# Channel shuffle in place: eight 24 KB buffers replaced by three 64 KB buffers with half-buffer stores

## The chip, the core and the metric

The kernel runs on one core of a Trainium2 chip. The metric is the device time of one execution in microseconds. A core has several engines that run side by side, each with its own instruction stream; here VectorE (DVE) and ScalarE (ACT) compute, and SyncE (SP) issues loads. ACT also issues the stores. The transfers themselves are done by 16 DMA engines, which take their work from one queue filled by SP and one filled by ACT.

## What is computed

The input has 16 x 64 x 64 rows of 256 channels in float32, 67.1 MB. In each row the 256 channels, 8 groups of 32, are transposed to 32 groups of 8. No arithmetic is done; every byte is read once from HBM and written once to it.

```
x = x.reshape(batch, h, w, groups, channels_per_group)   # groups 8, channels_per_group 32
x = x.transpose(0, 1, 2, 4, 3)
x = x.reshape(batch, h, w, c)
```

## The kernel before

A row of 256 channels is 1 KB, and there are 65,536 of them. A *tile* of size q is 128 x q consecutive rows: partition p holds the q rows that start at row p x q of the tile, so that each partition reads and writes one contiguous run of q KB. `_SIZES` (L12) lists 22 tiles: twenty of 24, one of 8, one of 24. They sum to 512, and 512 x 128 rows are the whole input.

Each tile takes one buffer of 24 KB a partition from a pool of eight (L13, L37, L49), 192 KB a partition in all. SP loads it with a single DMA (L50). Then, in pieces of 8 rows (8 KB a partition, `_PIECE`, L15), VectorE copies the piece to a PSUM tile called `bounce` and permutes it on the way (L54), and ScalarE copies `bounce` back over the same place in the buffer (L58). The PSUM pool has two such tiles. After the last piece of a tile, ACT issues a single DMA that stores the whole buffer (L59).

The instructions stand on each engine in the order in which they are written (the schedule is manual). Waits between engines are semaphores that the framework sets. SP can load tile i+8 when the store of tile i has landed, because it goes into the same buffer. All DMAs, loads and stores, share eight completion semaphores; a DMA that is to use one also waits until the DMA that used it before has landed. An engine that waits holds up everything behind it on its own stream: when ACT waits to issue a store, its next copies wait too, and with two PSUM tiles VectorE soon after.

Of the kernel before, what the change touches and what calls it, by code (L numbers as in the profile page):

```python
# [1 line left out]

# [4 lines left out]


F32 = mybir.dt.float32
P = 128  # L10

_SIZES = [24] * 20 + [8, 24]  # L12
_BUFS = 8  # L13

_PIECE = 8  # L15


@with_exitstack
def kernel(
    ctx: ExitStack,  # L20
    tc: tile.TileContext,
    x: bass.AP,
    groups: bass.AP,
    out: bass.AP,
):
    nc = tc.nc
    b, h, w, c = x.shape
    G = int(groups)
    CPG = c // G
    assert G * CPG == c  # L30
    assert sum(_SIZES) * P == b * h * w
    biggest = max(_SIZES)

    x_flat = x.rearrange("b h w c -> (b h w c)")
    out_flat = out.rearrange("b h w c -> (b h w c)")

    pool = ctx.enter_context(tc.tile_pool(name="pool", bufs=_BUFS))  # L37
    psum = ctx.enter_context(
        tc.tile_pool(name="psum", bufs=2, space=bass.MemoryType.PSUM)
    )  # L40

    def rows(flat, first, q):

        return flat[first * c : (first + P * q) * c].rearrange("(p f) -> p f", p=P)

    ctx.enter_context(tc.manual_schedule(engines=None))
    first = 0
    for q in _SIZES:
        buf = pool.tile([P, biggest * c], F32, name="buf")  # L49
        nc.sync.dma_start(out=buf[:, : q * c], in_=rows(x_flat, first, q))  # L50
        for k in range(0, q, _PIECE):
            piece = buf[:, k * c : (k + _PIECE) * c]
            bounce = psum.tile([P, _PIECE * c], F32, name="bounce")
            nc.vector.tensor_copy(  # L54
                out=bounce.rearrange("p (i j g) -> p i j g", j=CPG, g=G),
                in_=piece.rearrange("p (i g j) -> p i j g", g=G, j=CPG),
            )
            nc.scalar.copy(out=piece, in_=bounce)  # L58
        nc.scalar.dma_start(out=rows(out_flat, first, q), in_=buf[:, : q * c])  # L59
        first += P * q  # L60


# [1 line left out]
_INS = ['x', 'groups']  # L64
_OUTS = [((16, 64, 64, 256), 'float32')]

_NUMBERS = {'groups': 8}


# [26 lines left out]
```

## Time and profile before

| What | us |
|---|---|
| median of 4 runs | 317.55 |
| lowest and highest run | 317.46 and 317.63 |
| the profiled execution | 317.46 |
| its span, first to last recorded event | 315.7 |
| L54, VectorE copy, 64 of 3.637 us each | 227.9 busy, 72.2 idle before it |
| L58, ScalarE copy, 64 of 1.866 us each | 119.0 busy, 170.7 idle before it |
| L50, load of 3 MB, issue to landing, median of 21 | 59.4 |
| L59, store of 3 MB, issue to landing, median of 21 | 24.6 |
| first and last issue of a load | 0.7 and 241.8 |
| first and last issue of a store | 23.7 and 302.0 |

The profiled execution's time is 1.8 us more than its span; this much lies around what the profile records. The time from issue to landing of a DMA includes the time it stood in its queue behind earlier ones. The page gives a row of DMA shares, one digit for each of 40 slices of the span (9 is 90% or more of the 16 engines' time), and counts packets: a packet is what a DMA engine moves in one go. Besides the data, each DMA sends one packet of 4 bytes on each engine, which raises its completion semaphore. The view by windows cuts the span into stretches and gives the busy time and the number of instructions of each engine, the clock, the DMA share and the rate in GB/s of each; the DMA view does so for queues, where q1 holds the loads and q10 the stores. A packet is counted in the window in which it starts.

### The profile page before, as it was taken

The page shows a single profiled execution, that of the slowest core. Times are in us where ns is not written, and L with a number is a line of the kernel's source. Part 1 is how long each engine was busy: PE and PEld are TensorE (multiplying, and loading weights), DVE is VectorE, ACT ScalarE, POOL GpSimd, SP SyncE. Part 2 cuts the span into 40 slices and gives each one's busy share as a digit, 9 for nine tenths or more (in the row PEclk, how much of TensorE's full clock was granted, in tenths as well). Part 3 has the DMA queues.
Part 4 walks back from the last instruction along what each step waited for, and adds up shares of the span by engine and source line. Part 5 has one row for each costly group of instructions (what it writes and reads, how often), then busy time and mean ns, then how long its engine had stood idle before and what let it go on. Part 6 is the DMA issues. An engine that isn't in the chain of part 4 may idle for free.

```text
span 315.7 us, 289 instructions
## 1 busy us (share of the span) xinstructions
DVE 227.9 (72%) x64; ACT 120.3 (38%) x65; POOL 0.2 (0%) x4
## 2 busy tenths in 40 slices
DVE  0699999959586685957008986999970299999900
ACT  0354455524252424330015426545500444554420
POOL 0000000000000000000000000000000000000000
DMA  8999999999999999999999999999999999999997
GB/s 302 436 439 392 424 439 433 424 439 439 417 439 442 417 436 442 417 439 445 417 439 437 420 439 436 430 430 434 433 430 433 436 430 431 431 439 427 430 432 315
DMA packets 6338, 134.24 MB, mean 425 GB/s; under 512 B 704, under 2 KB 704, under 8 KB 704
## 3 DMA queue, kind: packets, MB, share of 16 engines
q1 hardware_dynamic: 3168, 67.11, 49.9%
q10 hardware_dynamic: 3168, 67.11, 49.4%
q14 instruction: 2, 0.02, 0.0%
HBM read 67.11 MB, written 67.11 MB: 425 GB/s over the span
## 4 chain that ended last, share of the span: by engine, by line
DVE 54%; another core or an unknown queue 23%; issue 8%; ACT 5%; DMA 3%; DVEq 1%; ACTq 0%
DVE bounce L54 54%; ACT buf L58 5%; DMA buf<-in_x_dram 3%; DVEq L91 1%; ACTq L59 0%; DVEq L54 0%; ACTq L58 0%
## 5 line engine op out<-in xcount | busy, mean ns | idle before, releaser
L54 DVE COPY bounce<-buf 128x2048 f32<-128x2048 f32 x64 | 227.9, 3637 | 72.2 <-ACT buf L58 38.4
L58 ACT COPY buf<-bounce 128x2048 f32<-128x2048 f32 x64 | 119.0, 1866 | 170.7 <-DVE bounce L54 115.3
L58 ACT ACT_TABLE_LOAD x1 | 1.3, 1283 | 11.1 <-DMA buf<-in_x_dram 11.1
L77 POOL MEMSET const-bfloat16-1.0<- 128x1 bf16 x1 | 0.1, 101 | 0.0
L77 POOL MEMSET const-uint8-127<- 128x1 uint8 x1 | 0.1, 101 | 0.0
L77 POOL MEMSET const-float32-0.0<- 128x1 f32 x1 | 0.1, 98 | 0.2 <-issue 0.2
L77 POOL MEMSET const-float32-1.0<- 128x1 f32 x1 | 0.1, 98 | 0.0
## 6 DMA issues: line engine op xcount, KB each, us to landing
buf<-in_x_dram SPq DMA_DIRECT2D x21, 3072.0 KB, 59.4
out_dram<-buf ACTq DMA_DIRECT2D x21, 3072.0 KB, 24.6
buf<-in_x_dram SPq DMA_DIRECT2D x1, 1024.0 KB, 44.9
out_dram<-buf ACTq DMA_DIRECT2D x1, 1024.0 KB, 16.1
```

What stands on the lines that cost most here:

```text
L54: nc.vector.tensor_copy(out=bounce.rearrange("p (i j g) -> p i j g", j=CPG, g=G), in_=piece.rearrange("p (i g j) -> p i j g", g=G, j=CPG),)
L58: nc.scalar.copy(out=piece, in_=bounce)
L77: nc = _bacc.Bacc("TRN2", target_bir_lowering=False, num_devices=1)
L91: with _tile.TileContext(nc) as tc:
```

## The change

The tiles become one of 16, one of 32, seven of 64 and one of 16 rows a partition (again 512 in all). The pool has three buffers of 64 KB a partition, again 192 KB. Each tile is still loaded by one DMA. The pieces stay 8 rows, and what VectorE and ScalarE do with a piece stays the same. A store now covers 32 rows (`_STORE`): ACT issues it after the copies of its four pieces, so that a tile of 64 is stored by two DMAs, the first while the second half is still to be permuted. There are 10 loads and 17 stores instead of 22 and 22.

```
-_SIZES = [24] * 20 + [8, 24]
-_BUFS = 8
+_SIZES = [16, 32] + [64] * 7 + [16]
+_BUFS = 3
+
+_STORE = 32
...
     for q in _SIZES:
         buf = pool.tile([P, biggest * c], F32, name="buf")
         nc.sync.dma_start(out=buf[:, : q * c], in_=rows(x_flat, first, q))
-        for k in range(0, q, _PIECE):
...
+        for a in range(0, q, _STORE):
+            b = min(a + _STORE, q)
+            for k in range(a, b, _PIECE):
+                piece = buf[:, k * c : (k + _PIECE) * c]
+                bounce = psum.tile([P, _PIECE * c], F32, name="bounce")
+                nc.vector.tensor_copy(
+                    out=bounce.rearrange("p (i j g) -> p i j g", j=CPG, g=G),
+                    in_=piece.rearrange("p (i g j) -> p i j g", g=G, j=CPG),
+                )
+                nc.scalar.copy(out=piece, in_=bounce)
+            cols = slice(a * c, b * c)
+            nc.scalar.dma_start(
+                out=rows(out_flat, first, q)[:, cols], in_=buf[:, cols]
             )
-            nc.scalar.copy(out=piece, in_=bounce)
-        nc.scalar.dma_start(out=rows(out_flat, first, q), in_=buf[:, : q * c])
         first += P * q
```

SP can now load tile i+3 when both stores of tile i have landed. The eight completion semaphores are shared as before.

More of the change, by code (lines that the diff above doesn't have):

```diff
@@ L26 @@
     nc = tc.nc
-    b, h, w, c = x.shape
+    n, h, w, c = x.shape
     G = int(groups)
@@ L30 @@
     assert G * CPG == c
-    assert sum(_SIZES) * P == b * h * w
+    assert sum(_SIZES) * P == n * h * w
     biggest = max(_SIZES)
@@ L50 @@
         nc.sync.dma_start(out=buf[:, : q * c], in_=rows(x_flat, first, q))
-        for k in range(0, q, _PIECE):
[L52 to L56, printed above, removed]
-            )
-            nc.scalar.copy(out=piece, in_=bounce)
-        nc.scalar.dma_start(out=rows(out_flat, first, q), in_=buf[:, : q * c])
+        for a in range(0, q, _STORE):
[11 more added lines that the diff above has]
+                out=rows(out_flat, first, q)[:, cols], in_=buf[:, cols]
+            )
         first += P * q
```

## The prediction

> **What bounds the kernel now.** I read the page first: busy shares, then the row of DMA shares, then the queues.
>
> ```profile
> span 315.7 us, 289 instructions
> DVE 227.9 (72%) x64; ACT 120.3 (38%) x65; POOL 0.2 (0%) x4
> ...
> DMA  8999999999999999999999999999999999999997
> ...
> DMA packets 6338, 134.24 MB, mean 425 GB/s; under 512 B 704, under 2 KB 704, under 8 KB 704
> ## 3 DMA queue, kind: packets, MB, share of 16 engines
> q1 hardware_dynamic: 3168, 67.11, 49.9%
> q10 hardware_dynamic: 3168, 67.11, 49.4%
> ```
>
> VectorE, the busiest engine, idles for 28% of the span; the DMA engines never do (two queues, 49.9% + 49.4%). The chain of waits ends on VectorE (54%) all the same, because it cannot see a queue that is merely full. The view by windows shows where DMA time is lost:
>
> ```profile
> core 0: us, DVE busy (x) ACT busy (x) POOL busy (x), PEclk, DMA share, GB/s
> 0.00:4.00 4.00, 0.00 (x0) 0.00 (x0) 0.20 (x4) 1.00 0.63 184
> 4.00:24.00 20.00, 12.96 (x4) 6.88 (x4) 0.00 (x0) 1.00 1.00 433
> 24.00:32.00 8.00, 8.00 (x3) 3.73 (x2) 0.00 (x0) 1.00 1.00 390
> 32.00:156.00 124.00, 92.98 (x27) 46.63 (x25) 0.00 (x0) 1.00 1.00 432
> 156.00:164.00 8.00, 0.00 (x0) 0.00 (x0) 0.00 (x0) 1.00 1.02 439
> 164.00:172.00 8.00, 5.32 (x2) 5.27 (x3) 0.00 (x0) 1.00 1.00 431
> ...
> 286.00:304.00 18.00, 14.12 (x4) 9.27 (x5) 0.00 (x0) 1.00 0.99 427
> 304.00:314.00 10.00, 0.00 (x0) 0.00 (x0) 0.00 (x0) 1.00 0.97 415
> 314.00:315.70 1.70, 0.00 (x0) 0.00 (x0) 0.00 (x0) 1.00 0.00 0
> ```
>
> The last column is the rate. It is about 432 GB/s with both queues (32 to 156), 433 with loads alone (4 to 24), and 431 with stores alone (the DMA view for 288 to 313.5). So 134.22 MB need 310.3 us, whichever queue supplies them. Losses are shortfalls against 432: (432 - 184)/432 x 4 = 2.3 us at the start, 0.8 us when the first store sets in (24 to 32), 0.2 + 0.4 us near the end, and 1.7 us after the last byte. 310.3 + 5.4 = 315.7, the span: nothing else is left to win.
>
> So the change can help only by cheaper bytes or smaller losses, and it hurts wherever **both** queues run empty at once. To foresee that I need the rule by which they share. The DMA view for 262 to 271, when an 8 KB tile loads beside 24 KB stores:
>
> ```profile
> DMA packets 264, 3.89 MB, mean 432 GB/s; under 512 B 21, under 2 KB 21, under 8 KB 21
> ## 3 DMA queue, kind: packets, MB, share of 16 engines
> q10 hardware_dynamic: 132, 2.85, 73.6%
> q1 hardware_dynamic: 132, 1.04, 27.3%
> ```
>
> 132 packets against 132: the queues take turns by packet, not by byte, and a packet is one partition's row. The queue with the longer rows gets more.
>
> **The change, part by part.**
>
> *Fewer, longer packets.* Now: (6338 - 704 - 2)/16 = 352 data packets an engine. Then: 10 loads and 17 stores, (10 + 17) x 128/16 = 216. In the view above, without the 4-byte ones, 1.04 MB are 127 packets of 8 KB and 2.85 MB are 116 of 24 KB. 8 KB takes 27.3% of 16 x 9 us by 127 = 309 ns; 24 KB takes 73.6% by 116 = 914 ns. Three times 309 is 927, so a packet has a fixed cost of (927 - 914)/2 = 6.5 ns; the shares sum to 100.9%, so the packets overlap a little and I take 5. 136 x 5 ns = **0.7 us less** (bounds 0 and 136 x 8 = 1.1).
>
> *DMA issues.* SP issues 10 loads of 0.33 us instead of 22, ACT 17 stores of 0.34 us instead of 22. Both wait most of the time: nothing.
>
> *Start.* Tiles of 16 and 32 rows are queued at once with the first 64: 14.7 MB, 34 us of transfers, so the queue is full whatever VectorE does. VectorE starts some 2.4 us earlier (1.05 MB less to wait for), which nothing awaits. The losses of 2.3 and 0.8 us stay.
>
> *Three buffers in place of eight.* Load i+3 waits on SP for both stores of tile i; behind it stand only later loads. With 64 KB against 32 KB rows, loads get two thirds (288 GB/s) and stores one third (144). One cycle, from the landing of a tile's second store: its buffer's new load (8.39 MB) takes 29.1 us, in which one half store (4.19 MB) passes; then the load queue is empty (no buffer free), and the next half store has the engines alone for 9.7 us. It frees the next buffer. That is 38.8 us a tile, exactly 16.78 MB at 432: no idle time. VectorE needs 8 x 3.56 = 28.4 us a tile (a step is 10.7/3), so it waits 10 us each cycle for a load, hidden by the transfers.
>
> *The end*, where the buffering decides. When the last 64-row load lands, three half stores are still unsent by that cycle: 12.6 MB. Behind them come the last load (2.1 MB) and the final stores. The last tile's first half is due at (12.6 + 2.1)/0.432 = 34 us after that landing and ready after 0.4 + 3.6 + 3 x 3.56 + 1.9 = 16.6 us (landing to VectorE, four copies, ACT's last); the second half due at 43.7, ready at 30.8; the last tile due at 53.4, ready at 37.9. A store needs some 1 to 4 us from issue to first byte (the first load's 1; the first store was issued at 23.7 and the dip ends by 29). Slack is 9 us or more everywhere: no gap.
>
> *A lost stall.* The chain shows "another core or an unknown queue" with 22.8%; its longest piece, 25.5 us before 164.3, is ACT holding a store for a DMA semaphore of an earlier transfer (eight are shared by all transfers). DMA ran at full share meanwhile, so dropping it returns nothing. In the new order the transfer that held the same semaphore is always long landed.
>
> *Restarts*, the unknown. The load queue now runs empty and starts again beside stores six times (every big tile but one, and the last). Before has no such restart. Nearest rows: the store queue's restart after 164 (431 against 432, under 0.1 us) and its first start (0.8 us). Six times that: 0 to 4.7 us; a gain is excluded, since a queue that starts adds no rate. I take 0, as a restart is like the row at 164, not like a first start.
>
> Sum: the profiled execution's 317.46 - 0.7 = 316.75. That execution lies 0.09 under the median of 317.55; I forecast **316.8**.
>
> *Two rules of the Trainium skill against rows.* The trace runs the only tile with a power-of-two row pitch, 8 KB, at 309 ns a packet, full rate. "DMA: Bandwidth & Descriptors", section "Latency and other measured facts", speaks against this change: copies lose rate at large power-of-two HBM row pitches, 207 GB/s at 512 KiB against 214 in full; 64 KB rows are new such pitches. Were that 3% paid here, the time would be about 327; at an eighth of that pitch I don't expect it, and no row here shows it. Its section "Bandwidth" gives 341 GB/s at 1 MB and 425 at 16 MB (transfers issued by GpSimd), which would promise much for larger DMAs; the rows here show 432 with 3 MB ones, since they queue back to back.
>
> **The rivals.**
>
> 1. *Slower: a 64 KB row is moved as two packets of 32 KB.* Rows up to 24 KB are one packet here; none of 64 KB is shown. Then the queues share equally, and loads no longer run ahead. The same bookkeeping leaves 6.2 MB unsent when the last big load lands; the last tile's second half is due at (6.2 + 2.1 + 4.2)/0.432 = 28.9 us but ready at 30.8 and on the wire 1 to 3 us later: 2.8 to 4.5 us with both queues empty. Net with 56 more packets: 317.5 + 2.8 or 4.5 - 0.4 = 319.8 to 321.5, likeliest 319.8. It decides as soon as less than some 8 MB is unsent then.
> 2. *Restarts cost part of the first start's price*, 0.1 to 0.8 us each: 317.3 to 321.4. Against it: the row at 164.
> 3. *Nothing measurable.* Packets have no fixed cost, or 0.3 us is lost elsewhere: 316.9 to 317.6. For it: 5 ns comes from a difference of 13 in 927.
> 4. *More than forecast.* Smaller first tiles also shrink the dip at the first store (0.8 us): 315.9 to 316.3.
>
> That the change doesn't do what it says is out: in the order of instructions every half store stands right after its fourth copy.
>
> **How the numbers follow.** No gap and packets cheaper, 316.3 to 317.1: 0.62. Rival 1: 0.12. Rival 2: 0.11. Rival 3: 0.07. Rival 4: 0.06. Rows above 24 KB, of which the trace shows none, move at a lower rate: 0.02. A measurement of this kernel tells about 0.2% (0.64 us) from no change, so the line lies at 316.9, inside the forecast's band: I count 0.45 of its 0.62 as faster. With rival 4 that makes 0.51. Same: the other 0.17, rival 3, 0.02 of rival 2: 0.26. Slower: 0.23. The range runs from rival 4's 315.9 to 320.0, leaving out the upper part of rivals 1 and 2; the restarts' far end, 321.4, lies in that part.
>
> **What would show it.** Right: 27 x 128 data packets; a big load landing some 29 us after it begins, and beside it twice the stores' bytes; load queue empty for some 10 us per tile; windows at 432 to 434 from 32 to 310; VectorE waiting for loads about 10 us a tile. Wrong: more packets with equal bytes in both queues and an empty slice near 298 (rival 1); dips each time a load follows stores alone (rival 2); under 430 throughout (long rows at a lower rate).

## The result, and the profile after

The changed kernel takes 317.89 us (median of 42 runs) where the kernel before takes 317.61 (63 runs beside it): a ratio of 1.0014, interval 1.0007 to 1.002. That is 0.3 us slower, where 0.8 us faster was forecast. It lies inside the bound of 0.2% that I had called "same", but on the wrong side of the ratio 1. The changed kernel's runs also lie further apart: 37 of them from 317.2 to 318.7 and five from 319.3 to 323.2, where before stays within 317.3 and 318.1. The run of 323.2 counts as slow, and the ratio leaves it out. The profiled execution took 317.88.

From the page of the changed kernel, the span, packets and queues:

```profile
span 316.1 us, 235 instructions
...
DMA packets 3890, 134.24 MB, mean 425 GB/s; under 512 B 432, under 2 KB 432, under 8 KB 432
## 3 DMA queue, kind: packets, MB, share of 16 engines
q1 hardware_dynamic: 1440, 67.11, 49.8%
q10 hardware_dynamic: 2448, 67.11, 49.2%
```

1440 load packets are 10 x (128 + 16): a row of 64 KB is one packet. (3890 - 432 - 2)/16 = 216 data packets an engine, as forecast. From the DMA view of the same kernel for 56 to 100 us:

```profile
q1 hardware_dynamic: 215, 13.04, 68.4%
q10 hardware_dynamic: 216, 6.03, 31.7%
```

215 packets against 216, and twice the bytes: the queues do take turns by packet. The chain of waits shows the cycle that follows from it (start, duration, what):

```profile
108.21 42.05 DMA out_dram<-buf
...
150.73 38.64 another core or an unknown queue
...
189.83 38.58 another core or an unknown queue
...
228.46 0.04 issue
228.50 32.99 DMA buf<-in_x_dram
```

Loads of big tiles are issued near 150.4, 189.5 and 228.5, some 39 us apart, where 38.8 was forecast. The schedule is the one that was forecast. Yet 0.7 us were to be won and 0.4 were lost in this execution (317.88 against 317.46). Where, the view by windows tells roughly and the DMA view exactly. First the windows, of before and then of after:

```profile
60.00:300.00 240.00, 178.80 (x51) 92.87 (x50) 0.00 (x0) 1.00 1.00 432
...
312.00:313.00 1.00, 0.00 (x0) 0.00 (x0) 0.00 (x0) 1.00 1.03 442
313.00:314.00 1.00, 0.00 (x0) 0.00 (x0) 0.00 (x0) 1.00 0.35 147
314.00:315.00 1.00, 0.00 (x0) 0.00 (x0) 0.00 (x0) 1.00 0.00 0
```

```profile
60.00:300.00 240.00, 188.57 (x54) 100.72 (x54) 0.00 (x0) 1.00 1.00 433
...
312.00:313.00 1.00, 0.00 (x0) 0.00 (x0) 0.00 (x0) 1.00 0.99 426
313.00:314.00 1.00, 0.00 (x0) 0.00 (x0) 0.00 (x0) 1.00 0.84 360
314.00:315.00 1.00, 0.00 (x0) 0.00 (x0) 0.00 (x0) 1.00 0.04 16
```

In the middle the changed kernel is a little faster, and at the end it is half a microsecond late all the same. So most was lost before 60 us. There the time of one load packet tells it: the share of the queue, times 16 engines and the window, over the data packets. Of the kernel before, the DMA view for 25 to 30 us and for 100 to 105:

```profile
q1 hardware_dynamic: 61, 1.45, 82.1%
...
q1 hardware_dynamic: 45, 1.11, 51.3%
```

1.45 MB are 59 packets of 24 KB, 0.821 x 80/59 = 1.11 us each; normal is 0.513 x 80/45 = 0.91. So each engine lost 0.20 x 59/16 = 0.74 us just after the first store: this is the dip that the prediction had seen. Of the changed kernel, 36 to 41, 46 to 54 and 64 to 72:

```profile
q1 hardware_dynamic: 18, 1.05, 55.8%
...
q1 hardware_dynamic: 32, 2.10, 74.6%
...
q1 hardware_dynamic: 36, 2.36, 68.0%
```

A 64 KB packet takes 2.79, 2.98 and (normal) 2.42 us: 16 and 32 packets with 0.37 and 0.56 us too much, 0.4 + 1.1 = **1.5 us** lost an engine instead of 0.74. The larger part comes after the load of 42.8 us, the first that is issued to a load queue already empty: its first restart. From 18 to 36 us, already beside the first store (issued at 17.5), a load packet takes the normal 2.42 (80.7% of 18 us for 96 packets); the smaller dip comes shortly before that store ends.

Five more restarts follow in this profile, and they cost nothing. For 154 to 162 us, after the load of 150.4:

```profile
q1 hardware_dynamic: 47, 3.08, 88.8%
```

That is 0.888 x 128/47 = 2.42 us a packet again; the windows after the other four give 2.42 and 2.43, and 0.61 for the last load's 16 KB.

### The profile page after: what moved, and what is told of

Its sections match the earlier page's. It is cut to its first block, busy times and chain, and to the rows that moved or that the text cites. A ratio compares the mean times of both kernels' runs of the same rounds, so it can differ in the third digit from the quotient of the medians.

```text
span 316.1 us, 235 instructions
## 1 busy us (share of the span) xinstructions
DVE 227.8 (72%) x64; ACT 120.7 (38%) x65; POOL 0.2 (0%) x4
## 2 busy tenths in 40 slices
DMA packets 3890, 134.24 MB, mean 425 GB/s; under 512 B 432, under 2 KB 432, under 8 KB 432
## 3 DMA queue, kind: packets, MB, share of 16 engines
q1 hardware_dynamic: 1440, 67.11, 49.8%
## 4 chain that ended last, share of the span: by engine, by line
DMA 45%; another core or an unknown queue 24%; DVE 21%; ACT 2%; DVEq 1%; issue 0%; SPq 0%
DMA buf<-in_x_dram 24%; DMA out_dram<-buf 21%; DVE bounce L58 21%; ACT buf L62 2%; DVEq L98 1%; SPq L52 0%; DVEq L58 0%
```

## The experiments

Names of the theories: **A**, the dip belongs to the first stores; **B**, a load queue that has run dry restarts unevenly beside stores; **C**, the dip belongs to a place in the load queue; **D**, chance; **L**, long packets cost by themselves.

**Both kernels once more**, without an edit.

> The kernel before, once more, for its profile. In the first profile 0.7 us of each DMA engine's time is lost to slow load packets between 26 and 29 us, just after the first store is issued (23.7). Theory A, the price belongs to the first store: the dip is there again, at 26 to 29 us, 0.6 to 0.8 us. Theory C, it belongs to a place in the load queue (its 26th to 31st packet on each engine): the same place and size. Theory D, it is chance: another place, or another size by more than 0.3 us.

> The changed kernel, once more, for its profile. In the first profile 1.6 us is lost in two dips, 0.4 us at 37 to 39 us and 1.2 us at 46 to 53 us, the latter where the load queue starts again beside stores for the first time. Theory B, the first restart costs about 1 us: the second dip is there again, after 46 us, 1.0 to 1.4 us. Theory C: both dips at the same load packets (26th, 28th and 29th). Theory D: they move, or change by more than 0.4 us.

Before: 317.46 again, the rate over 4 to 60 us 428 GB/s as in the first profile, and the dip in its old place and size (25 to 30 us: 79.2% for 57 data packets, 1.11 us each). After: 318.25, but lost elsewhere. The windows do not tell where: 60 to 300 us has 431 GB/s where the first profile had 433, but 4 to 60 has 437 where that had 425, and 4 to 300 has 432 in both. A packet is counted in the window in which it starts, and one more of 64 KB on each engine is 1 MB. The DMA view for 47 to 55 us, where the first restart falls, for 115 to 123 and for 232 to 240:

```profile
q1 hardware_dynamic: 32, 2.10, 62.5%
...
q1 hardware_dynamic: 32, 2.10, 62.1%
...
q1 hardware_dynamic: 35, 2.29, 66.2%
```

A load packet takes 2.50, 2.48 and 2.42 us. The first restart costs 0.2 us here, not 1.1; the three after it some 0.1 each (154 to 162 and 193 to 201 have 61.9% and 61.6% for 32 packets); the last two nothing. The dip at 36 to 41 is there again, 0.4 us. So B's figure for the second dip (1.0 to 1.4) did not come, and neither did C's; for that dip D holds.

What ends last in this profile is one engine. In 41 to 42 us 15 engines send the 4-byte packet that closes the third load, and one sends it in 43 to 44, before the first restart (load issued at 44.8). At the end, 314.5 to 315.5 us, one engine still begins a 16 KB packet when the 15 others have closed the last store:

```profile
q1 hardware_dynamic: 15, 0.00, 0.8%
...
q1 hardware_dynamic: 1, 0.00, 0.1%
...
DMA packets 2, 0.02 MB, mean 16 GB/s; under 512 B 1, under 2 KB 1, under 8 KB 1
```

Its last packet starts at 315.2 us, 0.9 after that of the next to last engine; in the first profile all 16 close the third load within 0.8 us. The record does not name the engines, so it is not shown that the late one is the same each time.

**The stores of the kernel before, three tiles late.**

```
     first = 0
+    late = []
...
-        nc.scalar.dma_start(out=rows(out_flat, first, q), in_=buf[:, : q * c])
+        late.append((rows(out_flat, first, q), buf[:, : q * c]))
+        if len(late) > 3:
+            to, of = late.pop(0)
+            nc.scalar.dma_start(out=to, in_=of)
         first += P * q
+    for to, of in late:
+        nc.scalar.dma_start(out=to, in_=of)
```

> The kernel before, with each store issued three tiles later, so that the first one goes out after the copies of the fourth tile, near 56 us instead of 23.7; the transfers stay the same and the queues stay full, so the time should be that of before within 0.3 us. Theory A: no dip at 26 to 29 us, and one of about 0.7 us at 57 to 62. Theory C: the dip stays at 26 to 29 us although no store is in flight. Theory D: a dip somewhere else.

317.67 us, ratio 0.9999 (0.999 to 1.0008). The DMA view for 25 to 30 us and for 54 to 59:

```profile
q1 hardware_dynamic: 94, 2.24, 103.8%
...
q1 hardware_dynamic: 63, 1.47, 82.5%
```

0.91 us a packet (91 of them carry data) and 1.10 (60): the dip has gone from 25 us and come to 54 with the first store, at the same price, 0.19 x 60/16 = 0.7 us. A holds for the kernel before; C falls.

**The changed kernel with each load in two.**

```
-        nc.sync.dma_start(out=buf[:, : q * c], in_=rows(x_flat, first, q))
+        for a in range(0, q, _STORE):
+            cols = slice(a * c, min(a + _STORE, q) * c)
+            nc.sync.dma_start(out=buf[:, cols], in_=rows(x_flat, first, q)[:, cols])
```

> The changed kernel with each load of 64 rows issued as two DMAs of 32 rows. Packets are then 32 KB on both queues, 256 and 16 an engine instead of 200 and 16; at 5 ns each that is 0.3 us more than the changed kernel. The queues share equally and the load queue never runs dry, since VectorE starts on the first half while the second is loading. Theory B: the 1.2 us of the first restart goes, so the time is about 0.9 us under the changed kernel's, near 317.0, 0.998 of before. Theory A: the time is that of before less 0.4 us, 317.2, with one dip of 0.7 us near 20 to 24 us. Theory C: a dip at the load queue's 26th to 31st packets, here at about 30 to 45 us, and the time 317.2 to 317.9. If the load packets of 64 KB themselves cost something, rates in the middle go from 434 to 433 and nothing else changes.

317.23 us, ratio 0.9993 (0.9981 to 1.0005), where the changed kernel has 1.0014 (1.0007 to 1.002). With neither 64 KB packets nor a dry queue, and 56 more data packets an engine (272 against 216), most of the loss is gone. A had said 317.2 and B 317.0, so the time does not tell them apart; the only dip is the one that A has, 0.5 us at 20 to 31 us (61.3% of 11 us for 82 packets, 1.32 us each instead of 1.21). In 60 to 300 us:

```profile
60.00:300.00 240.00, 178.02 (x51) 93.11 (x51) 0.00 (x0) 1.00 1.01 434
```

**Tiles of 48 in four buffers**, stored whole, and then in halves.

```
-_SIZES = [16, 32] + [64] * 7 + [16]
-_BUFS = 3
+_SIZES = [16, 32] + [48] * 9 + [16, 16]
+_BUFS = 4
-_STORE = 32
+_STORE = 48      # in the second version 24
```

> The changed kernel with nine tiles of 48 rows in four buffers (192 KB as before) instead of seven of 64 in three, each stored by one DMA. Both queues then have 48 KB packets and share equally; the load queue never runs dry. 208 data packets an engine, 0.7 us less than before. Theory B (a load queue that has run dry starts again beside stores unevenly, and the last of the 16 engines sets the end): nothing is given back, 316.9, 0.998 of before. Theory L (long packets are themselves uneven, dry queue or not): as the changed kernel, 317.7 to 318.2.

> The same tiles of 48 rows in four buffers, but stored in two DMAs of 24 rows each. Loads get two thirds again and the load queue runs dry eight times, some 8 us each. 288 data packets an engine, 0.3 us less than before. Theory B: eight restarts at 0.1 to 0.2 us give 0.8 to 1.6 us back, 318.1 to 318.9. Theory L: shorter store packets than in the version stored whole, so no worse than it plus 0.4 us. If neither costs anything: 317.3.

Whole: 320.21 us, 1.0078 (1.0052 to 1.0103); in halves: 318.36, 1.0031 (1.0015 to 1.0048). For the first, neither B's 316.9 nor L's 317.7 to 318.2 came, and it tells less than I wanted: in its profile (318.69) the store queue ran dry too, with no store packet from 287.1 to 289.3 us. The profiled execution of the second, 317.43, was its fastest, so it does not show what made the others slower. But it has the dry load queue eight times, and that cost it nothing. From 76.2 to 80.9 us only stores move; from 80 to 88, after the restart, a 48 KB load packet takes 0.683 x 128/48 = 1.82 us, as in a version below whose load queue does not run dry:

```profile
q10 hardware_dynamic: 88, 2.04, 100.7%
...
q1 hardware_dynamic: 48, 2.36, 68.3%
```

The windows after the next five restarts have 68.1% or 68.2% for 48 packets, and after the last two a 16 KB packet takes its normal 0.61 us. A restart beside stores need not cost anything.

**Tiles of 32 in six buffers.**

```
-_SIZES = [16, 32] + [64] * 7 + [16]
-_BUFS = 3
+_SIZES = [16] + [32] * 15 + [16]
+_BUFS = 6
```

> Fifteen tiles of 32 rows in six buffers (192 KB), each loaded and stored by one DMA, tiles of 16 first and last. 32 KB packets on both queues, 272 an engine, 0.4 us less than before; the load queue never runs dry. Theories B and L both: 317.2 to 317.4, 0.9985 to 0.999 of before, as with the changed kernel's split loads.

317.05 us, ratio 0.998 (0.9972 to 0.9989): this version beats both kernels. 434 GB/s in the middle, and the engines end together (0.99, then 0.12):

```profile
60.00:300.00 240.00, 178.00 (x51) 93.03 (x51) 0.00 (x0) 1.00 1.01 434
...
312.00:313.00 1.00, 0.00 (x0) 0.00 (x0) 0.00 (x0) 1.00 0.99 426
313.00:314.00 1.00, 0.00 (x0) 0.00 (x0) 0.00 (x0) 1.00 0.12 49
```

The price of a packet, 5 ns, had said 0.4 us less, and 0.6 came. The first dip is also smaller. For 16 to 32 us:

```profile
q1 hardware_dynamic: 187, 5.08, 76.9%
```

155 data packets of 1.27 us instead of 1.215 (100 to 116 us) are 0.5 us lost, where before loses 0.74. The two together account for the 0.6.

**One store per tile of 64** (`_STORE = 64` in the changed kernel).

> The changed kernel with one store of 64 rows per tile, issued after all eight pieces. Packets of 64 KB on both queues, 160 an engine, 0.9 us less than before. The bookkeeping of the prediction: the last big tile's store is ready only 30.8 us after its load lands, while all that is queued ahead of it is gone some 8 us earlier, so both queues are empty for 7 to 9 us near 290: 324 to 325.5. If the place of the stores does not matter, 317 to 318.

329.43 us, 1.0369 (1.0356 to 1.0383). The gap is where it was expected, and larger, (1 - 0.31) x 14 = 9.7 us in this window alone:

```profile
288.00:302.00 14.00, 14.00 (x5) 7.46 (x4) 0.00 (x0) 1.00 0.31 131
```

VectorE is busy all through it: the half-tile store is what hides the last tile's copies. In the changed kernel that slack was enough. Up to its first restart this version loads as the changed kernel does, and the restart cost as much again as in that kernel's first profile: 46 to 54 us has 77.1% for 32 load packets, 3.08 us each, 1.3 us lost.

**48 rows, with a big tile first** (`_SIZES = [48] * 10 + [24, 8]`).

> The version with tiles of 48 rows in four buffers stored whole, but with a tile of 48 first and the small ones (24, 8) last. The first store goes out near 42 us instead of 18, so more is loaded ahead and more stores stand in line at the end: by the bookkeeping neither queue runs dry after the first store, where the version with small tiles first let the store queue run dry near 283 us. 192 data packets an engine, 0.7 us less than before. Theory B (only restarts of a dry queue are uneven): nothing is given back, 316.6 to 317.1. Theory L (long packets are uneven by themselves): as slow as the version with small tiles first, 319 to 320.5, with a spread of some us between runs.

318.41 us, 1.0032 (1.0021 to 1.0043): between the two. I had left the loads only 2 us of margin, so it settled nothing, and another followed.

**Tiles of 32, stores in halves** (`_STORE = 16` in the version with six buffers; nothing else).

> Tiles of 32 rows in six buffers, with each store split in two of 16 rows: the load queue, with twice the stores' packet, runs dry nine times for 5.5 us each. 392 data packets an engine, 120 more than with whole stores, 0.6 us. Theory B: nine restarts at 0.1 to 0.2 us, 318.5 to 319.4. Theory L: short packets, so only the packets' price, 317.6 to 317.8, and runs as close together as with whole stores.

323.71 us, 1.0184 (1.0162 to 1.0206), far over both theories' figures. In the trace no load packet is under way from 118.6 to 124.3 us, nor in seven more stretches of 3 to 6 us up to 266. The windows:

```profile
60.00:120.00 60.00, 44.95 (x14) 23.51 (x13) 0.00 (x0) 1.00 1.00 433
120.00:270.00 150.00, 102.30 (x30) 52.71 (x30) 0.00 (x0) 1.00 1.01 422
...
314.00:316.00 2.00, 0.00 (x0) 0.00 (x0) 0.00 (x0) 1.00 0.88 377
316.00:318.00 2.00, 0.00 (x0) 0.00 (x0) 0.00 (x0) 1.00 0.35 147
318.00:320.00 2.00, 0.00 (x0) 0.00 (x0) 0.00 (x0) 1.00 0.31 131
```

Shares of 2:1 alone cost nothing (60 to 120: 433). With the restarts, 422: (433 - 422)/433 x 150 = 3.8 us, some 0.5 for each of the eight. And then the engines no longer end together: for the last 4 to 5 us only 0.35 and 0.31 of the 16 work, about five. The end of the kernel is the end of the latest engine. The DMA view for 80 to 88 and for 162 to 170 us, around a restart:

```profile
q1 hardware_dynamic: 70, 2.29, 66.3%
...
q1 hardware_dynamic: 59, 1.93, 62.3%
```

1.21 us a load packet before the first dry stretch, and 1.35 around the load issued at 160. In this kernel B holds: restarts cost, and they leave the engines apart.

**48 rows with margins** (`_SIZES = [40] + [48] * 9 + [24, 16]`, four buffers, stored whole).

> Tiles of 48 rows in four buffers, stored whole, with a first tile of 40 and last ones of 24 and 16. By the bookkeeping each load is issued at least 11 us before the load queue would run dry, and each store 5 us or more before the store queue would: the version with a first tile of 48 issued its loads only some 2 us ahead, and single engines ran dry. 192 data packets an engine, 0.7 us less than before. Theory B (the cost is the dry queue's restart): 316.7 to 317.1, and runs close together. Theory L (packets of 48 KB are uneven by themselves): 318 to 319, as with the first tile of 48.

318.56 us, 1.003 (1.0018 to 1.0042): the time is L's, not B's. Yet the middle is not slow, 433; the loss lies at both ends. Its DMA view, 35 to 43 us and 100 to 108, and its last windows:

```profile
q1 hardware_dynamic: 48, 2.36, 82.4%
...
q1 hardware_dynamic: 48, 1.57, 45.5%
```

```profile
312.00:313.00 1.00, 0.00 (x0) 0.00 (x0) 0.00 (x0) 1.00 0.69 295
313.00:314.00 1.00, 0.00 (x0) 0.00 (x0) 0.00 (x0) 1.00 0.43 180
314.00:315.00 1.00, 0.00 (x0) 0.00 (x0) 0.00 (x0) 1.00 0.08 33
```

2.20 us against 1.82 (48 and 32 data packets): the first store's dip costs 0.38 x 48/16 = 1.1 us with store packets of 40 KB beside loads of 48, not 0.74. (With the tile of 48 first, 42 to 46 us has 115.3% for 31 load packets, 2.38 us each: 1.1 us too.) And the engines end two to three microseconds apart. So what long packets cost lies at the first store and in engines that end apart, and not in the packets between.

**The kernel before with four and with five buffers** (`_BUFS = 4`, `_BUFS = 5`).

> The kernel before with four buffers instead of eight. Packets and shares stay equal, 24 KB. By the bookkeeping the load queue is dry for about 1 us in each of 18 cycles, and at the end both queues are empty for 5.3 us. Theory B: 317.6 + 5.3 + 18 restarts of 0.1 to 0.4 us = 324.7 to 330. Theory L: no long packets, 322.9.

> The kernel before with five buffers: each load is issued 15 us before the load queue would run dry, so no restarts; at the end both queues are empty for 4.4 us. Theories B and L: 317.6 + 4.4 = 322.0. What the four buffers cost beyond 0.9 us more than this is the restarts' price at equal packets.

325.89 us, 1.0258 (1.0242 to 1.0274), and 320.47, 1.0087 (1.0073 to 1.0101). Neither figure came. Windows of the four buffers:

```profile
60.00:300.00 240.00, 174.26 (x49) 91.44 (x49) 0.00 (x0) 1.00 1.00 432
300.00:316.00 16.00, 10.71 (x3) 5.60 (x3) 0.00 (x0) 1.00 0.45 191
```

Five buffers have 432 in the middle too. The dry moments of 1 us that I had worked out did not occur: from 60 to 290 us the trace of the four buffers has no stretch of half a microsecond without a load packet. All of the loss is the gap at the end, (1 - 0.45) x 16 = 8.8 us here, which my bookkeeping had put at 5.3. On B the pair has one thing: with four buffers the load queue ran dry once, from 38.4 to 44.4 us, and from 44 to 52 us, after the restart, a load packet takes the normal 0.570 x 128/80 = 0.91 us:

```profile
q1 hardware_dynamic: 80, 1.97, 57.0%
```

## Why the prediction was wrong, point by point

- **Packets.** 216 data packets an engine: right. That this is worth 0.7 us is not measured alone, but 434 and 433 GB/s against 432 in the middle, and the two versions with 32 KB packets, agree with it.
- **The bound**, "nothing else is left to win." Right only within 0.4 us: at the 432 GB/s that the prediction names, 134.22 MB need 310.7 us and not 310.3, and the losses then add up to more than the span. These 0.4 us are more than half of the gain that was forecast.
- **Sharing by packet, the cycle of 38.8 us, VectorE's waits** (9.7 to 10.6 us before five of the seven big tiles). Right, and Rival 1 is out: 64 KB is one packet. The 3% for a row pitch of 64 KB was not paid either: 433 GB/s in the middle.
- **The end.** Right: in 286 to 304 us the changed kernel's rate is 433, no gap. The version with one store a tile shows what the half stores are worth there.
- **The start**, "The losses of 2.3 and 0.8 us stay." Wrong for the second. The 0.8 is not a constant of the start: it belongs to the first store beside loads (the dip moved with it) and was 0.4 us at 36 to 41 here. That is the gain that Rival 4 had in mind; it was used up by the next term.
- **Restarts**, "I take 0, as a restart is like the row at 164, not like a first start." This is the step that failed. In the first profile the first of the six restarts cost 1.1 us, more than a first start (0.8), and the other five nothing; in the second profile four restarts cost 0.5 us together. It was listed as Rival 2, 317.3 to 321.4, where the measured 317.89 lies, with a chance of 0.11. The row at 164 was the *store* queue's restart beside loads, and I took it for the load queue's beside stores.
- **16 engines as one.** The sum has no term for an engine that falls behind the others, and in the second profile one was already 2 us late near 43 us, before any restart, and one ended 0.9 us after the rest.

The sum of the first profiled execution: -0.7 for packets, +0.8 for the early losses (1.5 - 0.74), which leaves +0.3 to come to the measured +0.4. The later end of single engines (0.84 against 0.35 of 16 in 313 to 314 us) accounts for about that, but the views do not part it further. Of the second: -0.7, and +0.2 for the slow packets (0.4 + 0.5 - 0.74), which leaves +1.3 to come to +0.8; the late engine is 0.9 of it, and the rest was not found.

What stays open: why one restart costs 1 us and another nothing. They were free in the version with 48 KB loads and 24 KB stores, dear with 32 and 16 KB, and with the same kernel the first one cost 1.1 and 0.2 us. How much of the changed kernel's loss over all its runs is restarts and how much late engines is not shown either: only two executions were profiled, and with three buffers of 64 KB I found no version that has long packets without the dry queue. Why a load slows when a store begins beside it, no view tells.

## What to carry to other kernels

When the DMA engines are busy all through, count bytes and packets first, and then ask not only whether a queue stays full on the average but whether either of them ever runs dry and starts again beside the other, and whether the 16 engines end together. The fewest packets were not the best here: 32 KB on both sides gained 0.2%, 48 KB on both sides with margins lost 0.3%, 64 against 32 KB lost 0.1%, 32 against 16 KB lost 1.8%. A row that stands in for one that the trace does not have must match it in direction too.

## What the runs showed of the hardware

Packets of the hardware queues take time by bytes plus a few ns (0.91 us for 24 KB, 1.21 for 32, 2.42 for 64), and two queues alternate packet by packet. The first store beside loads cost the engines 0.4 to 1.1 us on average. Here it went with the store's packets: 0.4 and 0.5 with 16 KB (beside loads of 64 and 32), 0.74 with 24, 1.1 with 40 and 48. A load queue that restarted beside stores cost anything from nothing (five of six in the changed kernel's first profile, all eight with 48 KB loads and 24 KB stores) to 1.3 us, and with 32 KB loads and 16 KB stores some 0.5 each time, which left the 16 engines up to 5 us apart. The program then pays for the latest engine in full.
